# Weighted sum over eight experts: a ring of nine slots in chunks of three, with a tail of two tokens

## The chip, the core and the metric

The kernel runs on one core of a Trainium2 chip. The metric is the device time in microseconds (us), the median of several executions. VectorE (DVE in the profile) does elementwise work, TensorE (PE) matrix products, ScalarE (ACT) and SyncE (SP) issue the transfers here, and 16 DMA engines carry them out.

## The reference

Sixteen thousand tokens each have eight vectors of 512 fp32 numbers, one per expert, and eight weights. The output is the weighted sum.

```python
batch, seq, n_experts, expert_dim = 16, 1024, 8, 512
weights = combine_weights[..., np.newaxis]
return np.sum(expert_outputs * weights, axis=2).astype(np.float32)
```

The input is 268.4 MB, the output 33.6 MB, the weights 0.5 MB. Each number of the input is used once.

## The kernel before

The 16384 tokens are laid over 128 partitions, so each partition has 128 tokens of its own (below, "token" is one such token on all partitions: 2.097 MB in, 0.262 MB out). The first 120 go through a loop, the last eight through a tail.

**The ring.** `ring` holds R = 10 tokens. A round n fills it once; there are twelve rounds. SyncE's queue (`loads_and_last_stores`) loads each round in three chunks, `CHUNKS`, of 4, 4 and 2 tokens (line 109). Before a chunk is loaded again, the queue waits on the semaphore `done`, which counts finished tokens (line 107), until the chunk's tokens of the round before are summed. Each chunk has its own semaphore `loaded`.

**DVE.** `terms` runs a hardware loop of six passes of two rounds (line 193). Per token there are eight instructions: a product with the first weight (line 204) and seven fused multiply-adds into `acc` (line 187). Two tokens are interleaved, so that an instruction does not follow straight on the one whose result it needs; each fused one waits on `step` for that result (line 209). At the start of a round DVE takes `w_set`, which tells that the round's weights are copied into `w_c`, and `stored`, which tells that this half of `acc` was stored two rounds ago; at the start of a chunk it takes `loaded`. `take` waits for a value and subtracts it (line 173).

**ScalarE.** `weights_and_stores` waits for the end of round n - 2, issues its store (line 99), and copies the weights of round n to `w_c` (line 145). After the loop it makes 32 diagonal matrices for the tail, in five buffers (line 151).

**The tail.** Eight tokens, loaded one by one (line 119) as DVE frees the first eight slots in the last round. PE sums the first four experts of each with diagonal weights into `ps` (line 163); DVE adds the other four, in `acc` (line 187). SyncE's queue then issues the store of the last round and four stores of the tail, of 4, 2, 1 and 1 tokens (line 123).

All instructions of one engine run in the order written. SyncE's and ScalarE's transfers stand in a DMA queue of each.

Of the kernel before, what the change touches and what calls it, by code (L numbers as in the profile page):

```python
# [10 lines left out]
def kernel(  # L11
# [14 lines left out]

    nc = tc.nc  # L30
    fp32 = mybir.dt.float32
    mult, add = mybir.AluOpType.mult, mybir.AluOpType.add

    B, S, E, D = expert_outputs.shape
    T = B * S
    P = 128
    R = 10
    G = 2 * R
    M = 2 * G
    T_P = T // P  # L40
    GROUPS = T_P // G
    LOOP = GROUPS * G
    TAIL = T_P - LOOP
    ROUNDS = LOOP // R
    CHUNKS = [(0, 4), (4, 4), (8, 2)]
    C = len(CHUNKS)
    DIAGS = 5

    x = expert_outputs.rearrange("b s e d -> (b s) e d")
    w = combine_weights.rearrange("b s e -> (b s) e")  # L50
    o = out.rearrange("b s d -> (b s) d")
    cut = LOOP * P
    x_g = x[0:cut].rearrange("(n p b g) e d -> n b p g e d", p=P, b=2, g=G)
    w_g = w[0:cut].rearrange("(n p m) e -> p n m e", p=P, m=M)
    o_g = o[0:cut].rearrange("(n p b g) d -> n b p g d", p=P, b=2, g=G)
    x_t = x[cut:T].rearrange("(p j) e d -> p j e d", j=TAIL)
    w_x = w[cut:T].rearrange("(p j) e -> p j e", j=TAIL)
    o_t = o[cut:T].rearrange("(p j) d -> p j d", j=TAIL)


    pe_e = [4] * TAIL
    tail_loads = [(j, 1) for j in range(TAIL)]
    tail_stores = [(0, 4), (4, 2), (6, 1), (7, 1)]

    order = []
    for q in ((0, 1), (2,), (3,), (4,), (5,), (6,), (7,)):
        order += [(j, e) for e in range(pe_e[q[0]], E) for j in q]
    diags = [(j, e) for j in range(TAIL) for e in range(pe_e[j])]

    one = ctx.enter_context(tc.tile_pool(name="one", bufs=1))  # L70
    psum = ctx.enter_context(tc.tile_pool(name="psum", bufs=1, space=bass.MemoryType.PSUM))
    ring = one.tile([P, R, E, D], fp32, name="ring")
    acc = one.tile([P, G, D], fp32, name="acc")
    w_t = one.tile([P, T_P, E], fp32, name="w_t")
    w_c = one.tile([P, G, E], fp32, name="w_c")
    ident = one.tile([P, P], fp32, name="ident")
    diag = one.tile([P, DIAGS, P], fp32, name="diag")
    ps = psum.tile([P, TAIL, D], fp32, name="ps")

    sem = tc.alloc_semaphore  # L80
    w_in = sem("w_in")
    w_set = [sem(f"w_set{h}") for h in range(2)]
    loaded = [sem(f"loaded{c}") for c in range(C)]
    stored = [sem(f"stored{h}") for h in range(2)]
    step = sem("step")
    done = sem("done")
    tail_in = [sem(f"tail_in{k}") for k in range(len(tail_loads))]
    tail_out = sem("tail_out")
    id_set = sem("id_set")
    diag_set = sem("diag_set")  # L90
    product = sem("product")

    def load_of(j):
        return [k for k, (q, m) in enumerate(tail_loads) if q <= j < q + m][0]

    def store(queue, n):
        h = n % 2
        queue.wait_ge(done, (n + 1) * R)
        queue.dma_start(
            out=o_g[n // 4, n // 2 % 2, :, h * R : h * R + R], in_=acc[:, h * R : h * R + R]  # L100
        ).then_inc(stored[h], 16)

    def loads_and_last_stores(sync):
        for n in range(ROUNDS):
            for c, (r, m) in enumerate(CHUNKS):
                if n:
                    sync.wait_ge(done, (n - 1) * R + r + m)
                g = n % 2 * R + r
                sync.dma_start(
                    out=ring[:, r : r + m], in_=x_g[n // 4, n // 2 % 2, :, g : g + m]  # L110
                ).then_inc(loaded[c], 16)
                if n == 0 and c == 0:
                    sync.dma_start(
                        out=w_t[:, 0:LOOP].rearrange("p (n m) e -> p n m e", m=M), in_=w_g
                    ).then_inc(w_in, 16)
                    sync.dma_start(out=w_t[:, LOOP:T_P], in_=w_x).then_inc(w_in, 16)
        for k, (j, m) in enumerate(tail_loads):
            sync.wait_ge(done, LOOP - R + j + m)
            sync.dma_start(out=ring[:, j : j + m], in_=x_t[:, j : j + m]).then_inc(tail_in[k], 16)
        store(sync, ROUNDS - 1)  # L120
        for j, m in tail_stores:
            sync.wait_ge(done, LOOP + j + m)
            sync.dma_start(out=o_t[:, j : j + m], in_=acc[:, j : j + m]).then_inc(tail_out, 16)
        sync.wait_ge(stored[(ROUNDS - 1) % 2], 16)
        sync.wait_ge(tail_out, 16 * len(tail_stores))

    def identity(gpsimd):
        gpsimd.memset(ident, 0.0).then_inc(id_set, 1)  # L128
# [10 lines left out]
    def weights_and_stores(scalar):  # L139
        scalar.wait_ge(w_in, 32)  # L140
        for n in range(ROUNDS):
            if n >= 2:
                store(scalar, n - 2)
            h = n % 2
            scalar.copy(  # L145
                out=w_c[:, h * R : h * R + R], in_=w_t[:, n * R : n * R + R]
            ).then_inc(w_set[h], 1)
        store(scalar, ROUNDS - 2)
        scalar.wait_ge(id_set, 2)
        for k, (j, e) in enumerate(diags):  # L150
            i = scalar.mul(out=diag[:, k % DIAGS], in_=ident, mul=w_t[:, LOOP + j, e : e + 1])  # L151
            i.then_inc(diag_set, 1)
            if k >= DIAGS:
                i.wait_op(product, k - DIAGS + 1, "sem-ge")

    def first_terms(tensor):
        came = set()
        for k, (j, e) in enumerate(diags):
            if load_of(j) not in came:
                came.add(load_of(j))  # L160
                tensor.wait_ge(tail_in[load_of(j)], 16)
            tensor.wait_ge(diag_set, k + 1)
            tensor.matmul(  # L163
                ps[:, j],
                lhsT=diag[:, k % DIAGS],
                rhs=ring[:, j, e],
                start=e == 0,
                stop=e == pe_e[j] - 1,
            ).then_inc(product, 1)

    def terms(vector):
        def take(s, v):
            vector.wait_ge(s, v).then_inc(s, -v)  # L173

        last = {}

        def count(i, g, e):

            if e == E - 1:
                i.then_inc(done, 1)  # L180
            else:
                i.then_inc(step, 1)
                last["all"] = last.get("all", 0) + 1
                last[g] = last["all"]

        def fused(g, e, weight, before):
            return vector.scalar_tensor_tensor(  # L187
                out=acc[:, g], in0=ring[:, g % R, e], scalar=weight, in1=before, op0=mult, op1=add
            )

        for h in range(2):
            vector.sem_inc(stored[h], 16)
        with nc.Fori(0, GROUPS, engines=OrderedEngineSet([vector.engine])):
            for h in range(2):
                take(w_set[h], 1)
                take(stored[h], 16)
                for c, (r, m) in enumerate(CHUNKS):
                    take(loaded[c], 16)
                    for q in range(h * R + r, h * R + r + m, 2):
                        for e in range(E):  # L200
                            for g in (q, q + 1):
                                weight = w_c[:, g, e : e + 1]
                                if e == 0:
                                    i = vector.tensor_scalar_mul(  # L204
                                        out=acc[:, g], in0=ring[:, g % R, 0], scalar1=weight
                                    )
                                else:
                                    i = fused(g, e, weight, acc[:, g])
                                    i.wait_op(step, last[g], "sem-ge")
                                count(i, g, e)  # L210
            take(step, last["all"])

        last.clear()
        came = set()
        take(stored[0], 16)
        vector.wait_ge(w_in, 32)
        for j, e in order:
            weight = w_t[:, LOOP + j, e : e + 1]
            if load_of(j) not in came:
                came.add(load_of(j))  # L220
                vector.wait_ge(tail_in[load_of(j)], 16)
            if e == pe_e[j]:
                i = fused(j, e, weight, ps[:, j])
                i.wait_op(product, sum(pe_e[: j + 1]), "sem-ge")
            else:
                i = fused(j, e, weight, acc[:, j])
                i.wait_op(step, last[j], "sem-ge")
            count(i, j, e)

    with tc.tile_critical(no_gpsimd_drain=True):  # L230
        loads_and_last_stores(nc.sync)
# [34 lines left out]
```

## Time and profile before

| what | value |
|---|---|
| time, median of 3 (range) | 707.9 us (707.88 to 708.25) |
| span of the profiled execution | 706.7 us |
| DVE, fused instruction in the loop (L187), mean | 744 ns, x840 |
| DVE, product with the first weight (L204), mean | 480 ns, x120 |
| DVE idle before L204, in all | 68.8 us, of which 25.1 at the start |
| load of the tail, issue to landing, median | 30.0 us |
| store of a round, issue to landing, median | 25.9 us |
| SyncE's queue waiting for DVE before the loads of the ring | 605.3 us in 33 waits |

A row of the groups gives the line, the engine, the operation, the tiles and the count, then busy time and the mean of one, then the idle time just before these instructions and what ended it. The mean of one is longer than the distance between two starts, since DVE starts an instruction while the one before is still ending. The table by stage has for each stretch the busy time of PE, weight loads, DVE, ACT and POOL, the clock of PE, the share of the time in which the DMA engines were busy, and GB/s. A share can come out a little over 1 as a packet's time and bytes are put down to one stretch.

### The profile page before, as it was taken

To read this page: it belongs to the slowest core of one execution; us is meant where nothing else is said; L and a number is where in the kernel's file an instruction comes from. 1 tells how busy PE (TensorE), PEld (TensorE's weight loads), DVE (VectorE), ACT (ScalarE), POOL (GpSimd) and SP (SyncE) were. 2 spreads that over 40 slices of the span, in tenths; PEclk is the share of its full clock that TensorE was granted. 3 is DMA by queue.
4 is the path that set the end of the run, shared out by engine and by line. 5 is a ranking of instruction groups with operands and counts; after the bars stand their busy time and mean duration, and the time that the engine had idled before them with its cause. 6 is when DMAs were issued, how large, how long until landed. Compare 5 with 4: busy or idle time off the path is not lost. (4 is left out here: it accounts for less than half of the span.)

```text
span 706.7 us, 1388 instructions
## 1 busy us (share of the span) xinstructions
PE 31.0 (4%) x64; PEld 12.2 (2%) x64; DVE 628.2 (89%) x992; ACT 16.7 (2%) x45; POOL 0.7 (0%) x6
## 2 busy tenths in 40 slices
PE   0000000000000000000000000000000000000664
PEld 0000000000000000000000000000000000000221
DVE  0599989979979979979989988998997997997994
ACT  0000000000000000000000000000000000000230
POOL 0000000000000000000000000000000000000000
PEclk9999999999999999999999999999999999999999
DMA  9999999999999999999999999999999999999997
GB/s 415 386 472 415 402 430 443 445 417 458 409 437 445 453 406 425 428 440 460 433 402 441 426 445 461 419 412 449 419 445 430 456 419 441 415 430 425 428 427 312
DMA packets 9186, 302.53 MB, mean 428 GB/s; under 512 B 1120, under 2 KB 1504, under 8 KB 1888
## 3 DMA queue, kind: packets, MB, share of 16 engines
q1 hardware_dynamic: 7600, 273.68, 89.9%
q10 hardware_dynamic: 1584, 28.84, 9.5%
q14 instruction: 2, 0.02, 0.0%
HBM read 268.96 MB, written 33.55 MB: 428 GB/s over the span
## 5 line engine op out<-in xcount | busy, mean ns | idle before, releaser
L187 DVE SCALAR_TENSOR_TENSOR acc<-ring,w_c,acc 128x512 f32<-128x512 f32 x840 | 561.4, 744 | 0.0
L204 DVE TENSOR_SCALAR acc<-ring,w_c 128x512 f32<-128x512 f32 x120 | 52.6, 480 | 68.8 <-DVEq L173 68.8
L163 PE MATMUL ps<-ring,diag 128*128 128x512 f32 x64 | 31.0, 631 | 667.0 <-DMA ring<-in_expert_outputs_dram 667.0
L163 PEld LDWEIGHTS ps<-ring,diag 128*128 128x128 f32 x64 | 12.2, 200 | 684.9 <-DMA ring<-in_expert_outputs_dram 672.4
L187 DVE SCALAR_TENSOR_TENSOR acc<-ring,w_t,acc 128x512 f32<-128x512 f32 x24 | 17.6, 751 | 0.6
L145 ACT COPY w_c<-w_t 128x80 f32<-128x80 f32 x12 | 3.0, 258 | 560.7 <-DVE acc L187 538.5
L151 ACT ACTIVATE diag<-ident,w_t 128x128 f32<-128x128 f32 x32 | 12.4, 399 | 114.4 <-PE ps L163 60.1
L187 DVE SCALAR_TENSOR_TENSOR acc<-ring,w_t,ps 128x512 f32<-128x512 f32 x8 | 5.9, 743 | 3.4 <-PE ps L163 3.4
L145 ACT ACT_TABLE_LOAD x1 | 1.3, 1283 | 0.9 <-SPq L230 0.9
L129 POOL TENSOR_SCALAR_AFFINE_SELECT ident<-ident 128x128 f32<-128x128 f32 x1 | 0.3, 292 | 0.1
L128 POOL MEMSET ident<- 128x128 f32 x1 | 0.2, 204 | 0.5 <-SPq L230 0.5
L250 POOL MEMSET const-bfloat16-1.0<- 128x1 bf16 x1 | 0.1, 102 | 0.0
L250 POOL MEMSET const-uint8-127<- 128x1 uint8 x1 | 0.1, 102 | 0.0
L250 POOL MEMSET const-float32-0.0<- 128x1 f32 x1 | 0.1, 99 | 0.2 <-issue 0.2
L250 POOL MEMSET const-float32-1.0<- 128x1 f32 x1 | 0.1, 99 | 0.0
## 6 DMA issues: line engine op xcount, KB each, us to landing
ring<-in_expert_outputs_dram SPq DMA_DIRECT2D x12, 4096.0 KB, 34.4
out_dram<-acc ACTq DMA_DIRECT2D x11, 2560.0 KB, 25.9
ring<-in_expert_outputs_dram SPq DMA_DIRECT2D x8, 2048.0 KB, 30.0
out_dram<-acc SPq DMA_DIRECT2D x1, 2560.0 KB, 26.2
out_dram<-acc SPq DMA_DIRECT2D x1, 1024.0 KB, 15.5
out_dram<-acc SPq DMA_DIRECT2D x1, 512.0 KB, 10.1
out_dram<-acc SPq DMA_DIRECT2D x2, 256.0 KB, 5.4
w_t<-in_combine_weights_dram SPq DMA_DIRECT2D x1, 480.0 KB, 22.6
```

The source lines that it names most:

```text
L128: gpsimd.memset(ident, 0.0).then_inc(id_set, 1)
L129: gpsimd.affine_select(out=ident, in_=ident, compare_op=mybir.AluOpType.not_equal, fill=1.0, base=0, pattern=[[-1, P]], channel_multiplier ...
L145: scalar.copy(out=w_c[:, h * R : h * R + R], in_=w_t[:, n * R : n * R + R]).then_inc(w_set[h], 1)
L151: i = scalar.mul(out=diag[:, k % DIAGS], in_=ident, mul=w_t[:, LOOP + j, e : e + 1])
L163: tensor.matmul(ps[:, j], lhsT=diag[:, k % DIAGS], rhs=ring[:, j, e], start=e == 0, stop=e == pe_e[j] - 1,).then_inc(product, 1)
L187: return vector.scalar_tensor_tensor(out=acc[:, g], in0=ring[:, g % R, e], scalar=weight, in1=before, op0=mult, op1=add)
L204: i = vector.tensor_scalar_mul(out=acc[:, g], in0=ring[:, g % R, 0], scalar1=weight)
L250: nc = _bacc.Bacc("TRN2", target_bir_lowering=False, num_devices=1)
```

## The change

The ring has nine slots and is filled in three equal chunks of three tokens. The loop holds two rounds, 18 tokens, and runs seven times, 126 tokens in 14 rounds. DVE interleaves the three tokens of a chunk instead of two. The tail shrinks from eight tokens to two, with accumulators of their own (`acc_t`), so that it need not wait for a store of the loop; PE sums five and four of their eight experts, with one buffer per diagonal. DVE no longer waits for stores: ScalarE waits for the store of round n - 2 to land before it copies the weights of round n, and DVE's wait for the weights covers both. SyncE's queue issues the stores of the last two rounds instead of the last one, after the tail's loads. A partition's tokens of the loop lie in one stretch of 63 instead of three of 40. The aim is a simpler and more even schedule, in which nearly all tokens go through the loop and DVE has one wait less.

```diff
-    R = 10
+    R = 9
+    C = 3
     G = 2 * R
-    M = 2 * G
+    M = 7 * R
...
-    CHUNKS = [(0, 4), (4, 4), (8, 2)]
-    DIAGS = 5
...
-    pe_e = [4] * TAIL
-    tail_loads = [(j, 1) for j in range(TAIL)]
-    tail_stores = [(0, 4), (4, 2), (6, 1), (7, 1)]
...
+    pe_e = [5, 4]
...
+    acc_t = one.tile([P, TAIL, D], fp32, name="acc_t")
...
-        store(sync, ROUNDS - 1)
-        for j, m in tail_stores:
-            sync.wait_ge(done, LOOP + j + m)
-            sync.dma_start(out=o_t[:, j : j + m], in_=acc[:, j : j + m]).then_inc(tail_out, 16)
...
+        for n in (ROUNDS - 2, ROUNDS - 1):
+            store(sync, n)
+        for j in range(TAIL):
+            sync.wait_ge(done, LOOP + j + 1)
+            sync.dma_start(out=o_t[:, j], in_=acc_t[:, j]).then_inc(tail_out, 16)
...
             if n >= 2:
                 store(scalar, n - 2)
+                scalar.wait_ge(stored[h], 16 * (n // 2))
             scalar.copy(
...
-        store(scalar, ROUNDS - 2)
...
-            for h in range(2):
-                take(w_set[h], 1)
-                take(stored[h], 16)
-                for c, (r, m) in enumerate(CHUNKS):
-                    take(loaded[c], 16)
-                    for q in range(h * R + r, h * R + r + m, 2):
-                        for e in range(E):
-                            for g in (q, q + 1):
...
+            for q in range(0, G, C):
+                if q % R == 0:
+                    take(w_set[q // R], 1)
+                take(loaded[q % R // C], 16)
+                for e in range(E):
+                    for g in range(q, q + C):
```

More of the change, by code (lines that the diff above doesn't have):

```diff
@@ L44 @@
     ROUNDS = LOOP // R
-    CHUNKS = [(0, 4), (4, 4), (8, 2)]
-    C = len(CHUNKS)
-    DIAGS = 5
+    assert LOOP % M == 0
     x = expert_outputs.rearrange("b s e d -> (b s) e d")
@@ L52 @@
     cut = LOOP * P
-    x_g = x[0:cut].rearrange("(n p b g) e d -> n b p g e d", p=P, b=2, g=G)
-    w_g = w[0:cut].rearrange("(n p m) e -> p n m e", p=P, m=M)
-    o_g = o[0:cut].rearrange("(n p b g) d -> n b p g d", p=P, b=2, g=G)
+    x_m = x[0:cut].rearrange("(n p k r) e d -> n k p r e d", p=P, k=M // R, r=R)
+    w_m = w[0:cut].rearrange("(n p m) e -> p n m e", p=P, m=M)
+    o_m = o[0:cut].rearrange("(n p k r) d -> n k p r d", p=P, k=M // R, r=R)
     x_t = x[cut:T].rearrange("(p j) e d -> p j e d", j=TAIL)
@@ L58 @@
     o_t = o[cut:T].rearrange("(p j) d -> p j d", j=TAIL)
-    pe_e = [4] * TAIL
-    tail_loads = [(j, 1) for j in range(TAIL)]
-    tail_stores = [(0, 4), (4, 2), (6, 1), (7, 1)]
-    order = []
-    for q in ((0, 1), (2,), (3,), (4,), (5,), (6,), (7,)):
-        order += [(j, e) for e in range(pe_e[q[0]], E) for j in q]
+    pe_e = [5, 4]
     diags = [(j, e) for j in range(TAIL) for e in range(pe_e[j])]
+    assert TAIL == len(pe_e)
     one = ctx.enter_context(tc.tile_pool(name="one", bufs=1))
@@ L76 @@
     ident = one.tile([P, P], fp32, name="ident")
-    diag = one.tile([P, DIAGS, P], fp32, name="diag")
+    diag = one.tile([P, len(diags), P], fp32, name="diag")
     ps = psum.tile([P, TAIL, D], fp32, name="ps")
@@ L82 @@
     w_set = [sem(f"w_set{h}") for h in range(2)]
-    loaded = [sem(f"loaded{c}") for c in range(C)]
+    loaded = [sem(f"loaded{c}") for c in range(R // C)]
     stored = [sem(f"stored{h}") for h in range(2)]
@@ L86 @@
     done = sem("done")
-    tail_in = [sem(f"tail_in{k}") for k in range(len(tail_loads))]
+    tail_in = [sem(f"tail_in{j}") for j in range(TAIL)]
     tail_out = sem("tail_out")
@@ L91 @@
     product = sem("product")
-    def load_of(j):
-        return [k for k, (q, m) in enumerate(tail_loads) if q <= j < q + m][0]
     def store(queue, n):
@@ L99, in store @@
         queue.dma_start(
-            out=o_g[n // 4, n // 2 % 2, :, h * R : h * R + R], in_=acc[:, h * R : h * R + R]
+            out=o_m[n * R // M, n % (M // R)], in_=acc[:, h * R : h * R + R]
         ).then_inc(stored[h], 16)
@@ L104, in loads_and_last_stores @@
         for n in range(ROUNDS):
-            for c, (r, m) in enumerate(CHUNKS):
+            for c in range(R // C):
+                r = c * C
                 if n:
-                    sync.wait_ge(done, (n - 1) * R + r + m)
-                g = n % 2 * R + r
+                    sync.wait_ge(done, (n - 1) * R + r + C)
                 sync.dma_start(
-                    out=ring[:, r : r + m], in_=x_g[n // 4, n // 2 % 2, :, g : g + m]
+                    out=ring[:, r : r + C], in_=x_m[n * R // M, n % (M // R), :, r : r + C]
                 ).then_inc(loaded[c], 16)
@@ L113, in loads_and_last_stores @@
                     sync.dma_start(
-                        out=w_t[:, 0:LOOP].rearrange("p (n m) e -> p n m e", m=M), in_=w_g
+                        out=w_t[:, 0:LOOP].rearrange("p (n m) e -> p n m e", m=M), in_=w_m
                     ).then_inc(w_in, 16)
                     sync.dma_start(out=w_t[:, LOOP:T_P], in_=w_x).then_inc(w_in, 16)
-        for k, (j, m) in enumerate(tail_loads):
-            sync.wait_ge(done, LOOP - R + j + m)
-            sync.dma_start(out=ring[:, j : j + m], in_=x_t[:, j : j + m]).then_inc(tail_in[k], 16)
-        store(sync, ROUNDS - 1)
-        for j, m in tail_stores:
-            sync.wait_ge(done, LOOP + j + m)
-            sync.dma_start(out=o_t[:, j : j + m], in_=acc[:, j : j + m]).then_inc(tail_out, 16)
-        sync.wait_ge(stored[(ROUNDS - 1) % 2], 16)
-        sync.wait_ge(tail_out, 16 * len(tail_stores))
+        for j in range(TAIL):
+            sync.wait_ge(done, LOOP - R + j + 1)
+            sync.dma_start(out=ring[:, j], in_=x_t[:, j]).then_inc(tail_in[j], 16)
+        for n in (ROUNDS - 2, ROUNDS - 1):
+            store(sync, n)
+        for j in range(TAIL):
+            sync.wait_ge(done, LOOP + j + 1)
+            sync.dma_start(out=o_t[:, j], in_=acc_t[:, j]).then_inc(tail_out, 16)
+        for h in range(2):
+            sync.wait_ge(stored[h], 16 * ROUNDS // 2)
+        sync.wait_ge(tail_out, 16 * TAIL)
     def identity(gpsimd):
@@ L141, in weights_and_stores @@
         for n in range(ROUNDS):
+            h = n % 2
             if n >= 2:
                 store(scalar, n - 2)
-            h = n % 2
+                scalar.wait_ge(stored[h], 16 * (n // 2))
             scalar.copy(
@@ L147, in weights_and_stores @@
             ).then_inc(w_set[h], 1)
-        store(scalar, ROUNDS - 2)
         scalar.wait_ge(id_set, 2)
         for k, (j, e) in enumerate(diags):
[L151 to L154, printed above, removed]
+            scalar.mul(
+                out=diag[:, k], in_=ident, mul=w_t[:, LOOP + j, e : e + 1]
+            ).then_inc(diag_set, 1)
     def first_terms(tensor):
-        came = set()
         for k, (j, e) in enumerate(diags):
-            if load_of(j) not in came:
-                came.add(load_of(j))
-                tensor.wait_ge(tail_in[load_of(j)], 16)
+            if e == 0:
+                tensor.wait_ge(tail_in[j], 16)
             tensor.wait_ge(diag_set, k + 1)
             tensor.matmul(
[L164 to L168, printed above, removed]
+                ps[:, j], lhsT=diag[:, k], rhs=ring[:, j, e], start=e == 0, stop=e == pe_e[j] - 1
             ).then_inc(product, 1)
@@ L184, in count, with fused @@
                 last[g] = last["all"]
-        def fused(g, e, weight, before):
+        def fused(out, x, weight, before):
             return vector.scalar_tensor_tensor(
-                out=acc[:, g], in0=ring[:, g % R, e], scalar=weight, in1=before, op0=mult, op1=add
+                out=out, in0=x, scalar=weight, in1=before, op0=mult, op1=add
             )
-        for h in range(2):
-            vector.sem_inc(stored[h], 16)
-        with nc.Fori(0, GROUPS, engines=OrderedEngineSet([vector.engine])):
-            for h in range(2):
-                take(w_set[h], 1)
-                take(stored[h], 16)
-                for c, (r, m) in enumerate(CHUNKS):
-                    take(loaded[c], 16)
-                    for q in range(h * R + r, h * R + r + m, 2):
-                        for e in range(E):
-                            for g in (q, q + 1):
[L202 to L210, printed above, removed]
@@ new lines, in terms @@
+        with nc.Fori(0, LOOP // G, engines=OrderedEngineSet([vector.engine])):
+            for q in range(0, G, C):
[4 more added lines that the diff above has]
+                    for g in range(q, q + C):
+                        x_e, weight = ring[:, g % R, e], w_c[:, g, e : e + 1]
+                        if e == 0:
+                            i = vector.tensor_scalar_mul(out=acc[:, g], in0=x_e, scalar1=weight)
+                        else:
+                            i = fused(acc[:, g], x_e, weight, acc[:, g])
+                            i.wait_op(step, last[g], "sem-ge")
+                        count(i, g, e)
@@ L211, in terms @@
             take(step, last["all"])
         last.clear()
[L214 to L228, printed above, removed]
+        for j in range(TAIL):
+            for e in range(pe_e[j], E):
+                x_e, weight = ring[:, j, e], w_t[:, LOOP + j, e : e + 1]
+                if e == pe_e[j]:
+                    i = fused(acc_t[:, j], x_e, weight, ps[:, j])
+                    i.wait_op(product, sum(pe_e[: j + 1]), "sem-ge")
+                else:
+                    i = fused(acc_t[:, j], x_e, weight, acc_t[:, j])
+                    i.wait_op(step, last[j], "sem-ge")
+                count(i, j, e)
```

## The prediction

> **What bounds the kernel now.** I read the busy shares first. VectorE (DVE) is busy 89% of the span, so it looks like the bound; but the DMA row of the slices stands at 9 from the first slice to the last but one, and the groups put 68.8 us of idle time in front of the first product of a token (line 204). DVE waits; the transfers don't.
>
> ```profile
> PE 31.0 (4%) x64; PEld 12.2 (2%) x64; DVE 628.2 (89%) x992; ACT 16.7 (2%) x45; POOL 0.7 (0%) x6
> ...
> DMA  9999999999999999999999999999999999999997
> ...
> HBM read 268.96 MB, written 33.55 MB: 428 GB/s over the span
> ```
>
> The table by stage gives the rate away from head and tail. Last column: GB/s, with the DMA share before it.
>
> ```profile
> 100.00:200.00 100.00, 0.00 (x0) 0.00 (x0) 95.32 (x152) 0.52 (x2) 0.00 (x0) 1.00 1.01 438
> 200.00:300.00 100.00, 0.00 (x0) 0.00 (x0) 91.96 (x147) 0.52 (x2) 0.00 (x0) 1.00 1.00 431
> 300.00:400.00 100.00, 0.00 (x0) 0.00 (x0) 92.71 (x148) 0.26 (x1) 0.00 (x0) 1.00 1.01 437
> ...
> 701.00:704.00 3.00, 0.00 (x0) 0.00 (x0) 0.10 (x1) 0.00 (x0) 0.00 (x0) 0.88 0.40 154
> ```
>
> In the middle the engines are full. Only after 701 us do they empty: 302.5 MB at about 435 GB/s is 695 us, so head and tail together cost some 11 us. Next, the timeline of DVE (start, duration, instructions, and in brackets the idle time before):
>
> ```profile
> 589.38 0.88 DVE L204 TENSOR_SCALAR acc<-ring,w_c 128x512 f32<-128x512 f32 x2 [4.05 <-DVEq L173]
> ...
> 643.80 0.88 DVE L204 TENSOR_SCALAR acc<-ring,w_c 128x512 f32<-128x512 f32 x2 [4.00 <-DVEq L173]
> 644.60 9.36 DVE L187 SCALAR_TENSOR_TENSOR acc<-ring,w_c,acc 128x512 f32<-128x512 f32 x14
> 653.88 0.88 DVE L204 TENSOR_SCALAR acc<-ring,w_c 128x512 f32<-128x512 f32 x2
> ```
>
> Two numbers come from here. A round of ten tokens takes 643.80 - 589.38 = 54.42 us; it moves 10 x (2.097 + 0.262) = 23.59 MB, so 433.5 GB/s. And starts run 0.80 us apart over two line-204 products and 9.28 us over fourteen fused ones: 0.40 us and 0.663 us each. Ten tokens are 80 instructions, 50.4 us; DVE has 4.0 us of slack per round, the bracket.
>
> The end is read on the tail's matmuls, which start when a tail token lands, and on the chain of waits.
>
> ```profile
> 678.62 3.70 PE L163 MATMUL ps<-ring,diag 128*128 128x512 f32 x8 [1.19 <-DMA ring<-in_expert_outputs_dram]
> 684.49 3.70 PE L163 MATMUL ps<-ring,diag 128*128 128x512 f32 x8 [2.16 <-DMA ring<-in_expert_outputs_dram]
> 689.39 3.70 PE L163 MATMUL ps<-ring,diag 128*128 128x512 f32 x8 [1.20 <-DMA ring<-in_expert_outputs_dram]
> 694.25 3.70 PE L163 MATMUL ps<-ring,diag 128*128 128x512 f32 x8 [1.16 <-DMA ring<-in_expert_outputs_dram]
> ```
>
> Tail tokens land 4.9 us apart, once 5.9 us: something held a DMA engine for 1.0 us there. The last one lands at 694.25; 3.7 us of matmul and four fused instructions follow, to 701.1; the span ends at 706.7. Meanwhile the last stores fill the DMA engines. The old tail is cut fine: after the last load only half a token is left for DVE and 256 KB to store.
>
> **What the Trainium skill says.** "DMA: Bandwidth & Descriptors", section "Where 436 GB/s comes from", gives 435.2 GB/s as the ceiling of a core's 16 DMA engines; the three stages above agree (431 to 438), so no arrangement of packets can gain in the middle. Its section "Queues, rings and completion order" says that an engine takes packets in turn from the queues that have work; the trace agrees, as a 2.56 MB store, 6.0 us of traffic alone, takes 25.9 us to land beside loads. "VectorE: DVE Perf Modes", on the TRN2 errata, prices a two-input fp32 instruction of 512 elements at 691 ns, and its 58 + N formula gives 594 ns; measured here are 663 ns between starts and 744 ns for one.
>
> **The change part by part.**
>
> *Chunks of three in nine slots.* The same bytes. A chunk is 6.29 MB, 14.5 us alone; a store of nine tokens 5.44 us; a round 49.0 us. When DVE frees a chunk, at least most of another is queued, so the DMA engines do not run dry: no change in the middle. The first chunk is smaller, so DVE starts some 5 us before its 25.07; nothing, as DVE waits in every round anyway.
>
> *DVE order in threes.* A chunk is 24 instructions: 3 x 0.40 + 21 x 0.663 = **15.1 us**. With two tokens interleaved, a fused instruction starts 1.33 us after the one that it waits for, which took 0.744: that wait does not bind, so a third token gains nothing. Per round 45.3 us against 49.0, slack 3.7 us. Bounds: 594 and 691 ns, so 13.7 to 15.7 us per chunk.
>
> *Waits of stores moved to ScalarE.* Behind them in its queue are the copy for round n (0.26 us) and the next store. A store should land about 21 us after its round ends (eight packets per engine in turn with eight longer ones of loads); the copy is wanted a whole round, 45 us or more, after that, and the next store too. Cost 0; hidden by a round of DVE work.
>
> *Weights, accumulators, diagonals.* Same bytes of weights in somewhat longer runs; under 0.5 us, taken as 0. The own accumulators free the tail of a wait for a store that landed some 29 us before it mattered: 0. PE has nine products instead of 32, over before DVE asks (below): 0.
>
> *The tail.* Here the bound changes. Two tail tokens replace eight. In the order of the SP queue come the loads, both tail loads, then the store of round 12, the store of round 13 and two of 256 KB.
>
> 1. When chunk 2 of round 12 lands, 117 tokens are loaded and 108 stored. At 694.25 the old kernel had 128 loaded and 110 stored: 23.07 + 0.52 = 23.59 MB more, 54.4 us. Without the 1.0 us hold: 694.25 - 1.0 - 54.4 = **638.9 us**. I take DVE to wait there, having caught up where a store stretches a load.
> 2. From there the SP queue holds back the store of round 12, so loads come every 14.5 us while DVE needs 15.1. DVE is the bound for four chunks: 638.9 + 4 x 15.1 = **699.3 us**.
> 3. The DMA engines meanwhile run out. Up to the end of the store of round 12 they move 117 stored tokens and all loads, 1.8 MB more than at the anchor: 693.3 + 4.2 = 697.5, less about 0.5 us between last byte and signal: 697. The store of round 13 is issued at 699.4 and its packets start about 1.0 us later, as after the first issue of the kernel (packets at 1.9 us, issue at 0.94). So some 3.4 us of idle DMA in front of the last 2.9 MB.
> 4. The store takes 5.44 us, to 705.8. DVE's seven tail instructions, 0.775 us apart as in the old tail, run till 704.8, so the two small stores follow without a gap: 1.3 us, 707.1. PE's last four products, 3.7 us after the second tail load at 692, are long done. From the last byte to the span's end the old trace has 1.9 us (last packet 704.8): **709.0 to 709.1**.
>
> Against 706.7 that is +2.4 us. The time: 707.9 + 2.4 = **710.3 us**.
>
> **The rivals.** *DMA alone sets the end* (no difference). If a chunk takes DVE under about 14.5 us, which the lower price of 594 ns allows, store 13 is issued before the engines run dry, and step 3's gap vanishes but for some start-up: about 2.2 us less, 708.1. For it: the price. Against: 663 ns held in every group of the old trace.
>
> *Faster.* As the last rival, and the DMA engine that lags is not held at the end: the old kernel's 1.0 us hold and the near-empty engines after 701 us are spared. 708.1 - 1.9 = 706.2. Against: 435 GB/s caps the rest, and nine slots leave DVE more work after the last loop load, not less.
>
> *Slower by the stream.* The same skill page, section "Latency and other measured facts", has 207 against 214 GB/s for partition rows 512 KiB apart, and worse for larger powers of two. Rows of the input now lie 63 x 16 = 1008 KiB apart, before 640 KiB. At the page's 3% it would be some 731 us. No run here shows a loss at 640 KiB, 1008 KiB is no power of two, and I take 0. A ring with one slot less could also run dry: 1 us per round would be 14 us, 724.
>
> **How the numbers follow.** Forecast 0.66, with one microsecond either way for DVE's rate (10 ns on a fused instruction move step 2 by 0.84 us) and for the lagging engine; DMA alone 0.14; faster 0.10; the stream slower 0.10. Low 707.0 leaves out the faster case, high 712.2 the slow stream and takes in 691 ns (4 x 0.6 = 2.4 us) nearly. Same (706.5 to 709.3): the 0.14 and some 0.05 of the forecast. Faster 0.11 with its edge, slower 0.70.
>
> **What would show it.** Right: a table by stage at 431 to 438 GB/s; DVE without a wait from the last chunk of round 12 to the tail; a dip in DMA share near 697 to 700 us, just before the last large store; stores landing after some 21 us. Wrong: waits of DVE in the last three chunks (the stream ends it), waits at ScalarE's copy (step of the stores), or fewer GB/s in the middle (pitch or ring).

## The result

The changed kernel takes 709.94 us (median of 6 runs, 709.61 to 710.39), the kernel before 707.97 us beside it: a ratio of 1.0029, 95% interval 1.0016 to 1.0042. It is slower by 2.0 us, where 2.4 us were forecast (710.3 us). The span of the profiled execution is 708.6 us against 706.7.

The page of the changed kernel looks as before, but for its ends:

```profile
PE 10.8 (2%) x18; PEld 4.4 (1%) x18; DVE 641.5 (91%) x1015; ACT 7.3 (1%) x24; POOL 0.7 (0%) x6
...
DMA  8999999999999999999999999999999999999996
...
HBM read 268.96 MB, written 33.55 MB: 427 GB/s over the span
...
DVE 9%; issue 0%; DVEq 0%
DVE acc L173 8%; DVE acc_t L173 1%; DVE acc L186 1%; DVEq L177 0%
```

The chain that ended last (the last two lines) holds no DMA at all any more. Before, 4% of the span in that chain was a load:

```profile
DMA 4%; DVE 3%; PE 1%; issue 0%
DMA ring<-in_expert_outputs_dram 4%; DVE acc L187 3%; PE ps L163 1%; DVE acc L204 0%
```

Both chains stop at DVE's last instruction; the stores behind it are not in them. The table by stage of the changed kernel (DMA share and GB/s are the last two columns) tells middle and end apart:

```profile
100.00:200.00 100.00, 0.00 (x0) 0.00 (x0) 92.97 (x149) 0.50 (x2) 0.00 (x0) 1.00 1.00 433
200.00:300.00 100.00, 0.00 (x0) 0.00 (x0) 92.97 (x149) 0.50 (x2) 0.00 (x0) 1.00 1.00 433
300.00:400.00 100.00, 0.00 (x0) 0.00 (x0) 92.96 (x149) 0.50 (x2) 0.00 (x0) 1.00 1.00 434
...
694.00:696.00 2.00, 2.00 (x6) 0.95 (x5) 2.00 (x4) 0.00 (x0) 0.00 (x0) 1.00 0.50 212
696.00:698.00 2.00, 1.61 (x4) 0.38 (x2) 2.00 (x4) 0.00 (x0) 0.00 (x0) 1.00 0.00 0
698.00:700.00 2.00, 0.00 (x0) 0.00 (x0) 1.97 (x4) 0.00 (x0) 0.00 (x0) 1.00 0.35 147
```

The middle runs at the rate of before. Between 694 and 700 us the DMA engines stand idle for 1.0 + 2.0 + 1.3 = 4.3 us, the mean of the 16, while DVE is busy. Then 2.9 MB of stores are still to come. The timeline of DVE shows why (start, duration, instructions, idle time before in brackets; `DVEq` stands for a wait in `take`):

```profile
622.58 1.28 DVE L186 TENSOR_SCALAR acc<-ring,w_c 128x512 f32<-128x512 f32 x3 [2.86 <-DVEq L159]
623.77 13.99 DVE L173 SCALAR_TENSOR_TENSOR acc<-ring,w_c,acc 128x512 f32<-128x512 f32 x21
638.42 1.28 DVE L186 TENSOR_SCALAR acc<-ring,w_c 128x512 f32<-128x512 f32 x3 [0.65 <-DVEq L159]
...
653.53 1.27 DVE L186 TENSOR_SCALAR acc<-ring,w_c 128x512 f32<-128x512 f32 x3
...
668.63 1.27 DVE L186 TENSOR_SCALAR acc<-ring,w_c 128x512 f32<-128x512 f32 x3
...
683.73 1.27 DVE L186 TENSOR_SCALAR acc<-ring,w_c 128x512 f32<-128x512 f32 x3
...
698.83 0.74 DVE L173 SCALAR_TENSOR_TENSOR acc_t<-ring,w_t,ps 128x512 f32<-128x512 f32 x1
...
701.83 2.33 DVE L173 SCALAR_TENSOR_TENSOR acc_t<-ring,w_t,acc_t 128x512 f32<-128x512 f32 x3
```

The last bracket is at 638.42, the last chunk of round 12. From there four chunks follow without a wait, 15.1 us each, to the first tail instruction at 698.83.

### The profile page after: what moved, and what is told of

Same layout as the page of the kernel before. It is cut to its first block, busy times and chain, and to the rows that moved or that the text cites. A ratio compares the mean times of both kernels' runs of the same rounds, so it can differ in the third digit from the quotient of the medians.

```text
span 708.6 us, 1280 instructions
## 1 busy us (share of the span) xinstructions
PE 10.8 (2%) x18; PEld 4.4 (1%) x18; DVE 641.5 (91%) x1015; ACT 7.3 (1%) x24; POOL 0.7 (0%) x6
## 5 line engine op out<-in xcount | busy, mean ns | idle before, releaser
L173 DVE SCALAR_TENSOR_TENSOR acc<-ring,w_c,acc 128x512 f32<-128x512 f32 x882 | 587.8, 744 | 0.0
L153 PE MATMUL ps<-ring,diag 128*128 128x512 f32 x18 | 10.8, 768 | 686.8 <-DMA ring<-in_expert_outputs_dram 686.8
L139 ACT COPY w_c<-w_t 128x72 f32<-128x72 f32 x14 | 3.4, 251 | 622.7 <-DMA out_dram<-acc 604.4
L153 PEld LDWEIGHTS ps<-ring,diag 128*128 128x128 f32 x18 | 4.4, 253 | 692.4 <-DMA ring<-in_expert_outputs_dram 686.8
L173 DVE SCALAR_TENSOR_TENSOR acc_t<-ring,w_t,acc_t 128x512 f32<-128x512 f32 x5 | 3.8, 752 | 0.2
L144 ACT ACTIVATE diag<-ident,w_t 128x128 f32<-128x128 f32 x9 | 2.7, 387 | 0.0
L173 DVE SCALAR_TENSOR_TENSOR acc_t<-ring,w_t,ps 128x512 f32<-128x512 f32 x2 | 1.5, 742 | 0.0
## 6 DMA issues: line engine op xcount, KB each, us to landing
out_dram<-acc ACTq DMA_DIRECT2D x12, 2304.0 KB, 23.2
```

What stands on the lines that cost most here:

```text
L139: scalar.copy(out=w_c[:, h * R : h * R + R], in_=w_t[:, n * R : n * R + R]).then_inc(w_set[h], 1)
L144: scalar.mul(out=diag[:, k], in_=ident, mul=w_t[:, LOOP + j, e : e + 1]).then_inc(diag_set, 1)
L153: tensor.matmul(ps[:, j], lhsT=diag[:, k], rhs=ring[:, j, e], start=e == 0, stop=e == pe_e[j] - 1).then_inc(product, 1)
L173: return vector.scalar_tensor_tensor(out=out, in0=x, scalar=weight, in1=before, op0=mult, op1=add)
```

## The experiments

Each ratio is to the kernel before, which took 707.9 us beside each; the edits are to the changed kernel (709.9 us).

**The store of round 12 back on ScalarE.** The gap in the DMA share invites the thought that the held-back store made it.

```diff
-        for n in (ROUNDS - 2, ROUNDS - 1):
-            store(sync, n)
+        store(sync, ROUNDS - 1)
...
+        store(scalar, ROUNDS - 2)
         scalar.wait_ge(id_set, 2)
```

> The store of round 12 goes back to ScalarE's queue, as the last but one store went before, and is issued when its round ends instead of behind the tail's loads. Theory 'DVE ends it' (four chunks of 15.1 us that DVE works off without a wait, because no store slows the loads there): the store now slows the loads of round 13 by its 5.4 us, DVE waits in round 13, ends later, and the last store with it: span about 3.7 us longer than the changed kernel's 708.6, so 712.3, time about 713.6. Rival 'the held-back store is what leaves the DMA engines idle': issued at once it fills nothing late, but the queue behind it is shorter by 5.4 us, so the time falls by up to 4 us, or stays.

Measured: 713.44 us, ratio 1.0076 (1.0063 to 1.0090); span 711.9. Its timeline of DVE has the waits of an ordinary round again in round 13:

```profile
671.13 1.28 DVE L186 TENSOR_SCALAR acc<-ring,w_c 128x512 f32<-128x512 f32 x3 [2.88 <-DVEq L159]
...
686.96 1.28 DVE L186 TENSOR_SCALAR acc<-ring,w_c 128x512 f32<-128x512 f32 x3 [0.65 <-DVEq L159]
...
702.06 0.74 DVE L173 SCALAR_TENSOR_TENSOR acc_t<-ring,w_t,ps 128x512 f32<-128x512 f32 x1
```

DVE reaches the tail 3.2 us later than in the changed kernel, and the span is 3.3 us longer. The early store takes time on the DMA engines from the loads that DVE needs last. So holding it back, one part of the change, is worth 3.5 us to the changed kernel (713.44 without it, 709.94 with it); it is not what costs.

**The last large store in three parts.** Each part is issued when its chunk of three tokens is summed.

```diff
-        for n in (ROUNDS - 2, ROUNDS - 1):
-            store(sync, n)
+        store(sync, ROUNDS - 2)
+        n = ROUNDS - 1
+        for c in range(R // C):
+            r = c * C
+            a = n % 2 * R + r
+            sync.wait_ge(done, n * R + r + C)
+            sync.dma_start(
+                out=o_m[n * R // M, n % (M // R), :, r : r + C], in_=acc[:, a : a + C]
+            ).then_inc(last_out, 16)
```

> The store of round 13 is issued in three parts of three tokens, each when its chunk is summed, instead of as one of nine tokens at the end. Theory 'DVE ends it': the idle DMA time before 699 us is filled by the first two parts, after DVE's last loop instruction only 0.8 MB and the tail's 0.5 MB are left; then the last tail store, issued after DVE's seven tail instructions, sets the end, so only about 0.9 us is gained: span 707.8, time about 709.1. Rival 'the last large store sets the end': all of its 3.6 us come off, time 706.3. Rival 'the stream is slower': no change, 709.9.

Measured: 709.0 us, ratio 1.0016 (1.0009 to 1.0022). Of the 3.6 us that two thirds of the store take, only 0.9 came off. The last tail instructions of DVE now gate the last small store: they run to 703.8 us, and the DMA engines are nearly idle from 702 to 704 us.

```profile
701.46 2.33 DVE L182 SCALAR_TENSOR_TENSOR acc_t<-ring,w_t,acc_t 128x512 f32<-128x512 f32 x3
...
702.00:704.00 2.00, 0.00 (x0) 0.00 (x0) 1.71 (x3) 0.00 (x0) 0.00 (x0) 0.50 0.17 64
```

**One instruction in eight left out of the loop.** The eighth expert is not added there, with all transfers kept.

```diff
-                for e in range(E):
+                for e in range(E - 1):
                     for g in range(q, q + C):
...
-                        count(i, g, e)
+                        count(i, g, e, E - 2)
```

> The loop leaves out the eighth expert, so its sums have seven terms; all loads and stores are as in the changed kernel. A chunk takes DVE 13.1 us instead of 15.1, less than its load of 14.5. Theory 'DVE ends it': the last store is issued before the DMA engines run dry, span about 3.2 us shorter, 705.4 to 705.6, time about 706.8, below the kernel before. Rival 'the stream is slower, by the row pitch, the packets of 48 KB or the smaller ring': transfers set the end whatever DVE does, time within 0.7 us of 709.9.

Measured: 706.8 us, ratio 0.9984 (0.9977 to 0.9991); span 704.9. DVE now waits before every chunk, to the last:

```profile
667.09 1.28 DVE L186 TENSOR_SCALAR acc<-ring,w_c 128x512 f32<-128x512 f32 x3 [1.34 <-DVEq L159]
...
681.62 1.28 DVE L186 TENSOR_SCALAR acc<-ring,w_c 128x512 f32<-128x512 f32 x3 [1.34 <-DVEq L159]
```

With the same bytes, packets, ring and row pitch it is 3.1 us faster than the changed kernel, and faster than the kernel before, which adds all eight terms. Its middle stages run at 433 GB/s, so the terms left out gain nothing there; what counts is DVE's work at the end. That excludes the stream as what made the change slower.

**DVE waits for the stores again.**

```diff
-                scalar.wait_ge(stored[h], 16 * (n // 2))
...
+        for h in range(2):
+            vector.sem_inc(stored[h], 16)
...
                     take(w_set[q // R], 1)
+                    take(stored[q // R], 16)
```

> One part of the change undone: DVE takes the semaphore of the stores itself, as before, and ScalarE copies weights without waiting for a store. Theory 'DVE ends it': the store lands some 23 us after its round ends, 25 us before anyone needs it, so the time stays at 709.9, within 0.5 us. Rival 'the wait on ScalarE costs': it falls by 1 us or more.

Measured: 710.01 us, ratio 1.0029 (1.0018 to 1.0039), against 709.94 us with ScalarE's wait. That wait costs nothing that can be told.

**More of the tail on PE.** Three kernels: `[6, 5]` and `[7, 6]`, both with the last large store in three parts as above, and `[7, 6]` with that store in one piece.

```diff
-    pe_e = [5, 4]
+    pe_e = [6, 5]
...
-    pe_e = [5, 4]
+    pe_e = [7, 6]
```

> The store of round 13 in three parts, and PE takes six and five of the tail tokens' experts instead of five and four, so DVE has five tail instructions instead of seven. Theory 'with the store in parts, DVE's tail instructions gate the last small store': two instructions of 0.775 us fewer, span 1.5 us under the kernel with the parts alone (707.3), 705.8, time about 707.4. Rival 'the transfers set the end once the store is in parts': no change from 709.0.

Measured (`[6, 5]`, in parts): 707.41 us, ratio 0.9993 (0.9985 to 1.0002).

> As the last, with seven and six experts on PE, so DVE has three tail instructions. Theory 'DVE's tail gates the end': PE's thirteen products, 0.86 us each after the first two, end near 699.7, DVE ends near 701.3 instead of 703.9: span about 704.9, time about 706.3, under the kernel before by 0.2%. Rival 'PE becomes the bound': its products end at 702 or later, and the time stays above 707.

Measured (`[7, 6]`, in parts): 707.34 us, from 706.38 to 707.98; ratio 0.9991 (0.9984 to 0.9997). The expectation missed by 1 us: in the profiled execution DVE waits for PE.

```profile
698.42 0.74 DVE L182 SCALAR_TENSOR_TENSOR acc_t<-ring,w_t,ps 128x512 f32<-128x512 f32 x1
700.93 0.75 DVE L182 SCALAR_TENSOR_TENSOR acc_t<-ring,w_t,ps 128x512 f32<-128x512 f32 x1 [1.76 <-PE ps L162]
```

An fp32 product here is two passes of PE, each with its own load of weights. The distance of these loads gives the time of a pass: 0.85 us at first and 0.43 us later.

```profile
690.83 0.34 PEld L162 LDWEIGHTS ps<-ring,diag 128*128 128x128 f32 x1 [0.52 <-issue]
691.68 0.34 PEld L162 LDWEIGHTS ps<-ring,diag 128*128 128x128 f32 x1 [0.52 <-issue]
...
693.43 0.19 PEld L162 LDWEIGHTS ps<-ring,diag 128*128 128x128 f32 x1 [0.24 <-issue]
693.86 0.19 PEld L162 LDWEIGHTS ps<-ring,diag 128*128 128x128 f32 x1 [0.24 <-issue]
```

The kernel with the store in parts alone had four slow passes; here there were seven. The Trainium skill, "TensorE: Matmul & The Clock Gate", section "What's actually happening", says that PE runs at half its clock until it has been busy through a window of about 3.4 us, and that these windows run freely, so that the number of slow products differs from run to run. Half the speed and the differing number agree with the traces; the slow stretch was about 3.4 us long with the store in parts alone and 6.1 us long here.

> Seven and six experts on PE, with the store of round 13 in one piece as in the changed kernel. Theory 'two limits behind one another': the store of nine tokens is issued at 699 and takes 5.4 us, the small ones follow it however early they are issued, so the time stays at 709.9, within 0.4 us. Rival 'DVE's tail is the limit in the changed kernel too': it falls by 2 us or more, to under 708.

Measured (`[7, 6]`, in one piece): 710.1 us, ratio 1.0031 (1.0018 to 1.0043). With the store whole, DVE's tail can end when it likes: the small stores stand behind 2.4 MB. The gain of [7, 6] exists only once the store is in parts, so two limits lie one behind the other.

**PE kept busy ahead of the tail.** To the kernel with [7, 6] and the store in parts:

```diff
     def first_terms(tensor):
+        tensor.wait_ge(w_in, 32)
+        tensor.wait_ge(id_set, 2)
+        tensor.wait_ge(done, LOOP - R + C)
+        for k in range(17):
+            tensor.matmul(
+                warm,
+                lhsT=ident,
+                rhs=w_t[:, 0 : D // E].rearrange("p a e -> p (a e)"),
+                start=True,
+                stop=True,
+            )
...
```

> The store of round 13 in three parts and seven and six experts of the tail on PE, with 17 more matrix products of no use (identity with weights, into a bank of their own) ahead of the tail's, from the end of the first chunk of round 13 on. Theory 'PE's slow first passes (0.86 us each, seven of them in the kernel without the extra products, then 0.43 us) made the second token's sum late': with PE busy beforehand all passes take 0.43 us, 26 of them end near 697.8, DVE no longer waits for PE and ends near 700.8 instead of 702.4, span about 704.9, time about 706.3, and the spread of 1.6 us between executions goes. Rival 'the transfers set the end at this point': time stays at 707.3.

Measured: 706.64 us (706.40 to 707.29), ratio 0.9983 (0.9976 to 0.9990); span 705.0. This beats both kernels, by 1.3 and 3.3 us. It is 0.3 us above what was expected, and the spread between executions fell from 1.6 to 0.9 us instead of going. PE's part of its timeline:

```profile
668.53 16.93 PE L163 MATMUL warm<-w_t,ident 128*128 128x512 f32 x34 [668.53 <-DVE acc L194]
686.50 11.43 PE L174 MATMUL ps<-ring,diag 128*128 128x512 f32 x26 [1.03 <-DMA ring<-in_expert_outputs_dram]
```

The 26 passes of the tail take 11.43 us, 0.44 each (14.49 us in the kernel without the extra products), and DVE's tail runs without a wait.

**Rows 2 MiB apart.** The changed kernel with another share-out of the tokens, to price what I had taken at zero. Weights and output are shared out in the same way, so rows of the output lie 256 KiB apart instead of 126.

```diff
-    x_m = x[0:cut].rearrange("(n p k r) e d -> n k p r e d", p=P, k=M // R, r=R)
...
+    x_p = x.rearrange("(p t) e d -> p t e d", p=P)
...
```

> The changed kernel with each partition's 128 tokens in one stretch, so that rows of the input lie 2 MiB apart (1008 KiB in the changed kernel, 640 KiB before), rows of the output 256 KiB; nothing else differs. Theory 'the DMA engines set the rate, not the pitch': middle stages at 433 to 435 GB/s, time within 1 us of 709.9. Rival 'a pitch of a large power of two costs' (the skill's DMA page has 164 against 214 GB/s at 2 MiB): 330 GB/s or so, time over 900 us.

Measured: 716.9 us, ratio 1.0133 (1.0117 to 1.0148): neither theory. Its table by stage:

```profile
0.00:50.00 50.00, 0.00 (x0) 0.00 (x0) 27.51 (x44) 1.69 (x3) 0.70 (x6) 1.00 0.97 397
...
200.00:300.00 100.00, 0.00 (x0) 0.00 (x0) 92.26 (x148) 0.50 (x2) 0.00 (x0) 1.00 1.00 432
300.00:400.00 100.00, 0.00 (x0) 0.00 (x0) 91.88 (x146) 0.50 (x2) 0.00 (x0) 1.00 1.00 428
```

The first 50 us run at 397 GB/s (417 in the changed kernel), the middle at 428 to 432 instead of 433 to 435. The whole kernel is 1.0% longer than with rows 1008 KiB apart. The stores' packets took 0.686 us as before, so the loss is in the loads: the median packet of 48 KB took 1.815 us in both kernels, but one in twenty took 1.98 us or more here, and 1.82 us in the changed kernel. The Trainium skill's figures in "DMA: Bandwidth & Descriptors", section "Latency and other measured facts" (164 against 214 GB/s, for copies from HBM to HBM), are far from this; it is also the section from which the prediction took its 3%. The measurement decides for loads to SBUF with runs of 48 KB. Why the loss is so small is open.

## Why the prediction was right, point by point

*The bound of before, and the middle.* Right: 433 to 435 GB/s after, and 431 to 438 before. The kernel with seven terms shows that neither ring, packets nor pitch cost anything that counts at the end.

*Chunks of three.* 15.1 us per chunk, as worked out; the third token interleaved gained nothing, a fused instruction still takes 744 ns and starts every 0.663 us (13.91 us over 21).

*ScalarE's wait.* Nothing, as the experiment with DVE waiting shows. The store lands 23.2 us after its issue, where I said 21. In the last round ScalarE copies the weights at 628.0 us, and DVE takes them at 653.5. (The store of before that I called 2.56 MB has 2560 KB, which is 2.62 MB; its 6.0 us are right.)

*Step 1* had DVE's last wait end at 638.9 us; it was 638.42. *Step 2* had 699.3 for the end of the loop; 698.83.

*Step 3* had the DMA engines empty at 697, the last store's packets from 700.4, and 3.4 us of idle time between. For the slowest of the 16 engines that is nearly so: its last packet ended at 696.7, and the store's first packets started at 699.8, 0.8 us after the issue at 698.94. But 13 engines were empty by 695.5, so the mean idle time was 4.3 us. The term that was off is the anchor: a load counts as landed when the slowest engine is done, and the others were ahead. It did not move the end, which hangs on when the store is issued.

*Step 4* had the last byte at 707.1 and the span's end at 709.0 to 709.1. The trace has the last packet's end at 706.8 and the span's end at 708.6. The forecast of the span was 0.4 us too long, about as much as step 1. PE's products ended at 697.6 instead of 695.7, since its first passes are slow; that was hidden behind DVE's loop, and became a wait only in the experiments that gave PE more.

*The rivals.* "DMA alone sets the end" and "faster" needed a chunk under 14.5 us, and the experiment with seven terms, at 13.2 us per chunk, ends at 706.8 us, between their 706.2 and 708.1. So their sums were sound; their premise, a fused instruction of 594 ns, was not: it is 663 ns between starts. "Slower by the stream" is excluded for this pitch, and even rows 2 MiB apart cost 7 us, a third of the 21 us that I had set against it.

*One account for all.* Adding up each trace's packets from 650 us to the last one gives the time for which the DMA engines stood idle at the end (mean of the 16). Taken off the span, it leaves nearly the same number for every kernel but one:

| kernel | span, us | idle at the end, us | difference, us |
|---|---|---|---|
| before | 706.7 | 2.3 | 704.4 |
| changed | 708.6 | 4.4 | 704.2 |
| store of round 12 on ScalarE | 711.9 | 7.8 | 704.1 |
| last large store in parts | 707.3 | 3.1 | 704.2 |
| seven terms | 704.9 | 0.6 | 704.3 |
| `[7, 6]`, in parts, PE kept busy | 705.0 | 0.7 | 704.3 |
| rows 2 MiB apart | 715.0 | 4.6 | 710.4 |

So the 1.9 us between the spans of before and after are idle time of the DMA engines at the end (2.1 us more of it), and none of them is a slower stream. Only the rows 2 MiB apart make the stream itself slower.

What stays open is how much of the 2.3 us of before is owed to the 1.0 us hold near 682 us, which the changed kernel does not show. That was not tried.

## What to carry to other kernels

In a stream that fills the DMA engines, an engine with 7% of slack on average can still set the end: ask where it waits for the last time, and add up its work from there. What is stored while the last loads run can delay these loads (3.5 us here); hold it back, and cut the very last store so that most of it goes while the compute engine still works. After each cut, find the next limit behind it before asking for the gain: here the store in parts was worth 0.9 us alone, more products on PE nothing alone, and both with PE kept busy 3.3 us.

## What the runs showed of the hardware

PE's slow start was worth 0.7 us of the kernel's time: a pass of an fp32 product of 512 columns took 0.85 us after a long idle time and 0.43 us after the first four to seven passes. With 34 passes ahead of them, 26 took 0.44 us on average, and the median fell from 707.34 to 706.64 us.

Pieces of 48 KB read from rows 2 MiB apart into SBUF came at 428 to 432 GB/s, about 1% slower than from rows 1008 KiB apart (433 to 435).

The 16 DMA engines do not finish together: at the end of the changed kernel's loads and held-back store, 13 were empty by 695.5 us and the last one at 696.7 us. The store counted as landed only at 697.1 us, after the slowest.
